# Two decoder layers on one core: small attention matmuls regrouped by the part of the array that they use

## The chip, the cores and the metric

The kernel runs on one core of one Trainium2 chip. The metric is device time in microseconds (us) from the launch to the end of the program; lower is better. Times come from several runs of the same kernel on the chip, and one further execution was recorded by the hardware profiler; the rows below are of that one. The core has a matrix engine (TensorE, PE in the profile, with its weight loads as PEld), a vector engine (DVE), a scalar engine (ACT), GpSimd (POOL) and a sync engine whose queue issues the DMAs (SP).

## What is computed

Two layers of a decoder on 512 prompt tokens and 8 x 4 sample tokens (544 columns in all, width 1024). Each layer is a half-step SwiGLU, a mixer of local attention and gated linear attention (GLA), cross attention to a memory of 256 rows, and a second half-step SwiGLU. The parts that matter here:

```python
def _swa_core(q, kc, vc, sinks, valid):      # 8 q heads, 2 kv heads, head dim 64, window 128
    s = einsum('bnqhgd,bnkhd->bnhgqk', q, kc) * HEAD_DIM ** -0.5
    s = where(valid, s, -inf)
    m = maximum(max(s, axis=-1), sink)
    e = exp(s - m)
    pr = e / (sum(e, axis=-1) + exp(sink - m))
    return einsum('bnhgqk,bnkhd->bnqhgd', pr, vc)

def step(S, inp):                            # GLA, 4 heads, dk 64, dv 128, chunks of 64 tokens
    ...
    A = where(causal, einsum('bhqd,bhkd->bhqk', q_t, k_t), 0.0)
    o = einsum('bhqd,bhdv->bhqv', q_t, S) + einsum('bhqk,bhkv->bhqv', A, vc)
    S_new = exp(b_last)[..., 0, :, None] * S + einsum('bhkd,bhkv->bhdv', k_dec, vc)
    return S_new, o

def cross_attn(h, mk, mv, p):                # 4 heads, head dim 128, 256 memory rows
    q = rms_norm((h @ p['xa_wq']).reshape(B, T, 4, 128), p['xa_q_norm'])
    a = softmax(einsum('bqhd,bkhd->bhqk', q, mk) * 128 ** -0.5)
    return einsum('bhqk,bkhd->bqhd', a, mv).reshape(B, T, 512) @ p['xa_wo']
```

The prompt attends to its own keys; each of the 8 samples has its own key cache, its own GLA state and its own memory keys and values.

## The kernel before

Activations lie transposed, features on the 128 partitions and the 544 tokens along the free axis. The large projections (`product`, line 222, and the feed-forward's `part`, line 447) split every operand in two fp32r halves and run as 128x128 by 272-column matmuls; ACT makes the high half of each weight tile (line 205 or 210) and DVE the low half (206, 211). The attention products are plain fp32; each such `pe.matmul` appears in the trace as two MATMUL records (transposes and fp32r matmuls as one).

The order of the steps in an attention phase is written out by hand in the lists `MIX` (mixer) and `CROSS`; `run` walks through them, and each `yield` in a step gives the next step its turn. The build then places the instructions on the engines by its own estimate of when operands and buffers are ready, so that a step's matmuls can be parted by others in the program that runs. PSUM tiles come from two pools: `psm()` gives a [128, 2, 512] tile of two banks (2 of them), `psa()` a [128, 512] tile of one bank (4 of them). SBUF tiles `big()` hold 4 x 544 columns (9 of them).

The steps that the change touches, all of them small products that use a part of the array's rows (contraction over 64 partitions) or of its columns (an output of 32 or 64 partitions):

- `swa_scores(l, n, kv, ...)`, called by `score n kv` for four windows n and two kv groups. Group kv lies on partitions 64*kv to 64*kv+63 of `qt` and `kt`; the four head blocks j of a group are four matmuls on the same 64 rows (line 536 for n = 0 with 128 columns, 542 else with 256). ACT copies one half of the result (537, 543), DVE masks in the other (538, 544), and then come the softmax, four transposes (565) and one or two masked copies `pt` (569).
- `swa_values`, called by `vals n`: per kv group, and per key block i, one matmul of 512 columns into partitions 64*kv to 64*kv+63 (580).
- `gla_prompt(n)`, called three times by `gla n`: masked products for heads on row half e (797), state updates for token half c (808; DVE adds them up in 815 and 818), and after a yield the outputs: per row half e and pair member i a full matmul with the masked product (834; for n = 0 two half-width ones, 837) and one per token half c with the state (842).
- `sample_scores` (`sscores` in `CROSS`): for each sample b four heads h, accumulated into the 32 columns of b (1237). The memory keys come by DMA, two samples in a `big()` tile (`streamed`, line 1200).
- `sample_values(g)` (`svals g`): for four samples e, two memory halves c, 512 columns each (1255); the values come by `streamed` too, two samples in a tile.

Of the kernel before, what the change touches and what calls it, by code (L numbers as in the profile page):

```python
# [84 lines left out]
def decoder_kernel(  # L85
# [436 lines left out]
        for _ in down(*prev, nxt):  # L522
            pass

    def swa_scores(l, n, kv, qt, kt, fq):


        sink, ns = col[:, l, C_SK + 4 * kv:C_SK + 4 * kv + 4], nsink[:, l, 4 * kv:4 * kv + 4]
        q0 = n * 128
        rows = slice(64 * kv, 64 * kv + 64)  # L530
        s = tmp("s")[:, :512].rearrange("p (j k) -> p j k", j=4)
        prev = km[:, M_PRV:M_PRV + 128].unsqueeze(1).to_broadcast([128, 4, 128])
        if n == 0:
            ps = psm()[:, 0].rearrange("p (j k) -> p j k", j=4)
            for j in range(4):
                pe.matmul(ps[:, j, :], qt[rows, j, 0:128], kt[rows, 0:128], start=True, stop=True)
            act.copy(out=s, in_=ps)
            dve.copy_predicated(out=s, mask=prev, data=neg.unsqueeze(1).to_broadcast([128, 4, 128]))
# [6 lines left out]
        yield 1  # L545
        sm = smp.tile([128, 4, 4], F32, tag="sm", name="sm")
        nm, es, su = sm[:, 0, :], sm[:, 1, :], sm[:, 2, :]
        dve.tensor_reduce(out=es, in_=s, axis=AX.X, op=ALU.max)
        f = fq[:, n, :].rearrange("p (j e) -> p j e", e=2)[:, :, kv]
        dve.scalar_tensor_tensor(out=nm, in0=es, scalar=-1.0, in1=f, op0=ALU.mult, op1=ALU.mult)  # L550
        dve.tensor_tensor(out=nm, in0=nm, in1=ns, op=ALU.min)
# [5 lines left out]
        dve.tensor_tensor(out=es, in0=nm, in1=sink, op=ALU.add)  # L557
# [15 lines left out]
        return out  # L573

    def swa_values(n, pts, vtok, ah, al):
        o = psa()
        for kv in range(2):
            rows = slice(64 * kv, 64 * kv + 64)
# [73 lines left out]
    def mixer(l, nx, nxt):  # L652
# [136 lines left out]
        def gla_prompt(n):  # L789
            st = held["st"]  # L790
            c0 = n * 128
            a = am[n % 2]
            for e in range(2):
                rows = slice(64 * e, 64 * e + 64)
                ps = psa()[:, 0:256].rearrange("p (i t) -> p i t", i=2)
                for i in range(2):
                    pe.matmul(ps[:, i, :], k_t[i][rows, c0:c0 + 128], q_t[i][rows, c0:c0 + 128], start=True, stop=True)
                dve.copy_predicated(
                    out=a[:, 2 * e:2 * e + 2, :],
                    mask=km[:, M_GLA:M_GLA + 128].unsqueeze(1).to_broadcast([128, 2, 128]), data=ps,  # L800
                )
            states = []
            for c in range(2):
                tok = slice(64 * c, 64 * c + 64)
                up = psa()[:, 0:256].rearrange("p (i v) -> p i v", i=2)
                for h in range(4):
                    rows = slice(64 * (h % 2), 64 * (h % 2) + 64)
                    pe.matmul(
                        up[rows, h // 2, :], ktok[tok, n, 64 * h:64 * h + 64], vgt[tok, n, h, :],
                        start=True, stop=True,  # L810
                    )
# [12 lines left out]
            if n == 3:  # L824
                nc.sync.dma_start(out=o_sp[l].rearrange("(i h) d v -> (h d) i v", i=2), in_=st)
            yield 1
            os = []
            for e in range(2):
                rows = slice(64 * e, 64 * e + 64)
                o = psa()[:, 0:256].rearrange("p (i v) -> p i v", i=2)  # L830
                os.append(o)
                for i in range(2):
                    if n > 0:
                        pe.matmul(o[:, i, :], a[:, 2 * e + i, :], vgt[:, n, 2 * i + e, :], start=True, stop=False)  # L834
                    for c in range(2):
                        if n == 0:
                            pe.matmul(
                                o[64 * c:64 * c + 64, i, :], a[:, 2 * e + i, 64 * c:64 * c + 64],
                                vgt[:, n, 2 * i + e, :], start=True, stop=c == 0, tile_position=(0, 64 * c),
                            )  # L840
# [164 lines left out]

        probs = {}

        def scores(n, kv):
            probs[n, kv] = yield from swa_scores(l, n, kv, qt, kt, held["fq"])

        def values(n):
            swa_values(n, [probs[n, 0], probs[n, 1]], vtok, ah, al)
# [145 lines left out]
    def cross(l, nx, nxt):  # L1158
# [70 lines left out]

        def sample_scores():  # L1230
            ps = psa().rearrange("p (g s) -> p g s", g=2)
            for b in range(NB):
                if b % 2 == 0:
                    kt = streamed(cmk_t[l, b // 2], u=4)
                r = slice(32 * (b % 4), 32 * (b % 4) + 32)
                for h in range(4):
                    pe.matmul(  # L1237
                        ps[r, b // 4, :], held["xbd"][:, h, b, :], kt[:, b % 2, h, :], start=h == 0, stop=h == 3,
                        tile_position=(0, 32 * (b % 4)),
                    )  # L1240
# [5 lines left out]
        def sample_values(g):  # L1246
            pts, (oh, ol) = held["sturn"], outs()
            o = psa()
            for e in range(4):
                b = 4 * g + e  # L1250
                if b % 2 == 0:
                    vt = streamed(cmv[l, b:b + 2].rearrange("b (c s) w -> s b c w", c=2), u=2)
                r = slice(32 * e, 32 * e + 32)
                for c in range(2):
                    pe.matmul(  # L1255
                        o[r, :], pts[:, (2 * g + c) * 128 + 32 * e:(2 * g + c) * 128 + 32 * e + 32],
                        vt[:, b % 2, c, :], start=c == 0, stop=c == 1, tile_position=(0, 32 * e),
                    )
            yield 1
            ob = tmp("z")[:, 0:512]  # L1260
# [224 lines left out]
```

## Time and profile before

| | us |
|---|---|
| median of 3 runs | 2222.85 (2221.82 to 2223.49) |
| profiled execution, its own time | 2225.04 |
| span of the profiled execution, first to last instruction | 2223.2 |
| PE busy | 2199.3 (99%) |
| DVE busy | 1567.8 (71%) |
| ACT busy | 1050.1 (47%) |
| mean granted TensorE clock | 0.994 |

The profile's page gives the busy time of each engine, a chain of work followed back from the last instruction, and groups of instructions by line. The chain can be asked for any stretch; its pieces then follow each other without overlap, so a piece's length is the time for which these instructions held up the rest. A busy time of PE also counts the tail of a matmul that overlaps the next one, and is somewhat larger. The two layers show the same picture: mixer and cross attention run from about 400 to 724 us and from about 1500 to 1825 us.

### The profile page before, as it was taken

The page shows a single profiled execution, that of the slowest core. Times are in us where ns is not written, and L with a number is a line of the kernel's source. Part 1 is how long each engine was busy: PE and PEld are TensorE (multiplying, and loading weights), DVE is VectorE, ACT ScalarE, POOL GpSimd, SP SyncE. Part 2 cuts the span into 40 slices and gives each one's busy share as a digit, 9 for nine tenths or more (in the row PEclk, how much of TensorE's full clock was granted, in tenths as well). Part 3 has the DMA queues.
Part 4 walks back from the last instruction along what each step waited for, and adds up shares of the span by engine and source line. Part 5 has one row for each costly group of instructions (what it writes and reads, how often), then busy time and mean ns, then how long its engine had stood idle before and what let it go on. Part 6 is the DMA issues. An engine that isn't in the chain of part 4 may idle for free.

```text
span 2223.2 us, 40766 instructions
## 1 busy us (share of the span) xinstructions
PE 2199.3 (99%) x17250; PEld 2113.1 (95%) x17250; DVE 1567.8 (71%) x2467; ACT 1050.1 (47%) x1721; POOL 7.0 (0%) x17
## 2 busy tenths in 40 slices
PE   8999999999999999999999999999999999999999
PEld 8999999988897999999999999999878979999999
DVE  7987786537654797877679787764476457977874
ACT  6544443535455644444455444435455555444441
POOL 0000000000000000000000000000000000000000
PEclk8999999999999999999999999999999999999999
DMA  4333323322244233233223332333222532333232
GB/s 184 116 94 96 105 86 111 95 75 85 81 149 174 77 105 105 86 105 96 77 85 97 109 91 95 105 100 102 62 87 86 198 116 87 104 97 104 86 101 73
DMA packets 74999, 227.07 MB, mean 102 GB/s; under 512 B 7713, under 2 KB 19745, under 8 KB 73505
## 3 DMA queue, kind: packets, MB, share of 16 engines
q1 hardware_dynamic: 74816, 224.47, 31.6%
q8 instruction: 135, 2.21, 0.4%
q14 instruction: 48, 0.39, 0.1%
HBM read 214.64 MB, written 9.04 MB: 101 GB/s over the span
## 4 chain that ended last, share of the span: by engine, by line
PE 96%; ACT 2%; DVE 1%; DMA 0%; issue 0%; SPq 0%; DVEq 0%; ACTq 0%
PE pm L222 48%; PE pa L447 36%; PE pm L1121 1%; PE pm L1083 1%; PE pm L542 1%; PE pa L580 1%; PE pa L1237 1%; PE pa L1255 1%; PE pa L842 1%; PE pa L1223 1%; PE pa L917 0%; PE pa L834 0%; ACT s L1135 0%; PE pa L565 0%; PE pa L264 0%
## 5 line engine op out<-in xcount | busy, mean ns | idle before, releaser
L222 PE MATMUL pm<-big,hi 128*128 128x272 f32 x5760 | 803.4, 292 | 14.5 <-DVE z L376 10.4
L222 PEld LDWEIGHTS pm<-big,hi 128*128 128x128 f32 x5760 | 757.5, 191 | 21.0 <-issue 13.3
L222 PE MATMUL pm<-big,lo 128*128 128x272 f32 x2880 | 420.5, 289 | 0.0
L222 PEld LDWEIGHTS pm<-big,lo 128*128 128x128 f32 x2880 | 383.0, 188 | 2.1 <-issue 1.2
L205 ACT CAST hi<-raw 128x1024 fp32r<-128x1024 f32 x196 | 205.4, 1049 | 248.6 <-PE pm L222 136.7
L206 DVE TENSOR_TENSOR lo<-raw,hi 128x1024 fp32r<-128x1024 f32 x196 | 238.7, 1218 | 51.9 <-PE pm L222 29.6
L210 ACT CAST hs<-sum 128x1024 fp32r<-128x1024 f32 x152 | 159.9, 1052 | 173.2 <-PE pa L447 143.8
L447 PE MATMUL pa<-t,hs 128*128 128x272 f32 x1368 | 238.7, 289 | 0.0
L447 PE MATMUL pa<-big,hs 128*128 128x272 f32 x1064 | 211.1, 288 | 0.0
L447 PEld LDWEIGHTS pa<-t,hs 128*128 128x128 f32 x1368 | 201.0, 188 | 0.0
L211 DVE TENSOR_TENSOR ls<-sum,hs 128x1024 fp32r<-128x1024 f32 x152 | 185.3, 1219 | 1.8 <-ACT hs L210 0.5
L447 PE MATMUL pa<-big,hi 128*128 128x272 f32 x1216 | 178.7, 289 | 0.0
L387 DVE SCALAR_TENSOR_TENSOR x<-pm,x 128x544 f32<-128x544 f32 x192 | 138.3, 720 | 45.6 <-PE pm L222 45.4
L447 PEld LDWEIGHTS pa<-big,hs 128*128 128x128 f32 x1064 | 166.6, 189 | 0.0
L447 PEld LDWEIGHTS pa<-big,hi 128*128 128x128 f32 x1216 | 163.0, 188 | 0.0
L447 PE MATMUL pa<-t,ls 128*128 128x272 f32 x912 | 153.0, 290 | 0.0
L447 PEld LDWEIGHTS pa<-t,ls 128*128 128x128 f32 x912 | 129.7, 189 | 0.0
L210 ACT CAST hi<-raw 128x1024 fp32r<-128x1024 f32 x76 | 80.1, 1054 | 96.5 <-PE pm L222 84.7
L210 ACT CAST hd<-raw 128x512 fp32r<-128x512 f32 x76 | 47.2, 621 | 138.0 <-PE pa L447 131.5
L447 PE MATMUL pa<-big,lo 128*128 128x272 f32 x608 | 109.5, 288 | 0.0
L433 DVE TENSOR_TENSOR sum<-raw 128x512 f32<-128x512 f32 x152 | 98.2, 686 | 12.7 <-DMA raw<-in_wts_dram 12.7
L433 DVE TENSOR_TENSOR sum<-sum,raw 128x512 f32<-128x512 f32 x152 | 104.2, 686 | 0.0
(303 smaller groups left out, 2609.3 us busy)
## 6 DMA issues: line engine op xcount, KB each, us to landing
raw<-in_wts_dram SPq DMA_DIRECT2D x348, 512.0 KB
big<-in_cmk_t_dram SPq DMA_DIRECT2D x8, 1024.0 KB
big<-in_cmv_dram SPq DMA_DIRECT2D x8, 1024.0 KB
kc<-in_consts_dram SPq DMA_DIRECT2D x2, 1546.0 KB
x<-in_x_dram SPq DMA_DIRECT2D x8, 272.0 KB
z<-big SPq DMA_DIRECT2D x32, 68.0 KB
out_dram<-x SPq DMA_DIRECT2D x8, 272.0 KB
cache<-in_s_dram SPq DMA_DIRECT2D x8, 256.0 KB
```

The lines of the kernel that those rows point to most:

```text
L205: act.copy(out=hi, in_=raw)
L206: dve.tensor_tensor(out=lo, in0=raw, in1=hi.bitcast(F32), op=ALU.subtract)
L210: act.copy(out=hi, in_=src)
L211: dve.tensor_tensor(out=lo, in0=src, in1=hi.bitcast(F32), op=ALU.subtract)
L222: pe.matmul(ps[:, h, :s.stop - s.start], w, x[:, s], start=i == 0, stop=i == len(steps) - 1)
L387: dve.scalar_tensor_tensor(out=x, in0=p, scalar=scale, in1=x, op0=ALU.mult, op1=ALU.add)
L433: dve.tensor_tensor(out=t[:, e], in0=t[:, 0] if x is None else x, in1=y, op=ALU.add)
L447: pe.matmul(ps, u, v, start=first and i == 0, stop=i == len(steps) - 1, skip_group_check=not first)
L542: pe.matmul(ps[:, j, :], qt[rows, j, q0:q0 + 128], kt[rows, q0 - 128:q0 + 128], start=True, stop=True)
L580: pe.matmul(o[rows, :], vtok[:, n - i, rows], p, start=i == 0, stop=i == len(pts[kv]) - 1)
L842: pe.matmul(o[64 * c:64 * c + 64, i, :], q_t[i][rows, c0 + 64 * c:c0 + 64 * c + 64], states[c][rows, i, :], start=False, stop=True, tile_p ...
L1083: pe.matmul(pk[:, h, :], w[:, o:o + 128], x[:, k, :], start=st and h % 2 == 0, stop=sp and h % 2 == 1)
```

## The change

Five places, with the same operands and results:

- `swa_scores` takes a pair of head blocks w in place of a kv group: blocks 2w and 2w+1, each for both kv groups e. Its four matmuls alternate between row halves 0 to 63 and 64 to 127, and e picks the PSUM bank. The factors, sinks and the copies after it are addressed accordingly; for n = 0 the tile takes both banks.
- `swa_values` makes twice as many matmuls of 256 columns, alternating between the column halves.
- `gla_prompt` issues the masked products alternating between row halves; the state updates alternate between token halves and column halves; in the outputs both row halves' tiles `os` are taken first, and for each i the full matmuls of both e come first, then the four with the states.
- `sample_scores` takes the key tiles of four samples first, then goes over heads h with the four samples inside, each on its own 32 columns.
- `sample_values` takes both value tiles first, then goes over c with the four samples inside.

```diff
-    def swa_scores(l, n, kv, qt, kt, fq):
+    def swa_scores(l, n, w, qt, kt, fq):
...
+        ps = psm().rearrange("p e (j k) -> p j e k", j=2)
+        for j in range(2):
+            for e in range(2):
+                rows = slice(64 * e, 64 * e + 64)
+                pe.matmul(
+                    ps[:, j, e, 0:q0 + 128 - k0], qt[rows, 2 * w + j, q0:q0 + 128], kt[rows, k0:q0 + 128],
+                    start=True, stop=True,
+                )
         if n == 0:
-            ps = psm()[:, 0].rearrange("p (j k) -> p j k", j=4)
-            for j in range(4):
-                pe.matmul(ps[:, j, :], qt[rows, j, 0:128], kt[rows, 0:128], start=True, stop=True)
-            act.copy(out=s, in_=ps)
+            act.copy(out=s, in_=ps[:, :, :, 0:128])
...
         else:
-            ps = psm().rearrange("p a (j k) -> p (a j) k", j=2)
-            for j in range(4):
-                pe.matmul(ps[:, j, :], qt[rows, j, q0:q0 + 128], kt[rows, q0 - 128:q0 + 128], start=True, stop=True)
-            act.copy(out=s, in_=ps[:, :, 128:256])
-            dve.copy_predicated(out=s, mask=prev, data=ps[:, :, 0:128])
+            act.copy(out=s, in_=ps[:, :, :, 128:256])
+            dve.copy_predicated(out=s, mask=prev, data=ps[:, :, :, 0:128])
...
     def swa_values(n, pts, vtok, ah, al):
         o = psa()
-        for kv in range(2):
-            rows = slice(64 * kv, 64 * kv + 64)
-            for i, p in enumerate(pts[kv]):
-                pe.matmul(o[rows, :], vtok[:, n - i, rows], p, start=i == 0, stop=i == len(pts[kv]) - 1)
+        for w in range(2):
+            for i, p in enumerate(pts[w]):
+                for kv in range(2):
+                    rows = slice(64 * kv, 64 * kv + 64)
+                    pe.matmul(
+                        o[rows, 256 * w:256 * w + 256], vtok[:, n - i, rows],
+                        p.rearrange("p (j e q) -> p e j q", j=2, e=2)[:, kv], start=i == 0, stop=i == len(pts[w]) - 1,
+                    )
...
-            for e in range(2):
-                rows = slice(64 * e, 64 * e + 64)
-                ps = psa()[:, 0:256].rearrange("p (i t) -> p i t", i=2)
-                for i in range(2):
+            halves2 = [slice(0, 64), slice(64, 128)]
+            pss = [psa()[:, 0:256].rearrange("p (i t) -> p i t", i=2) for _ in range(2)]
+            for i in range(2):
+                for ps, rows in zip(pss, halves2):
                     pe.matmul(ps[:, i, :], k_t[i][rows, c0:c0 + 128], q_t[i][rows, c0:c0 + 128], start=True, stop=True)
...
-            os = []
-            for e in range(2):
-                rows = slice(64 * e, 64 * e + 64)
-                o = psa()[:, 0:256].rearrange("p (i v) -> p i v", i=2)
-                os.append(o)
-                for i in range(2):
+            os = [psa()[:, 0:256].rearrange("p (i v) -> p i v", i=2) for _ in range(2)]
+            for i in range(2):
+                for e, o in enumerate(os):
                     if n > 0:
                         pe.matmul(o[:, i, :], a[:, 2 * e + i, :], vgt[:, n, 2 * i + e, :], start=True, stop=False)
...
+                for c, tok in enumerate(halves2):
+                    for e, o in enumerate(os):
                         if states[c] is not None:
                             pe.matmul(
-                                o[64 * c:64 * c + 64, i, :], q_t[i][rows, c0 + 64 * c:c0 + 64 * c + 64],
-                                states[c][rows, i, :], start=False, stop=True, tile_position=(64 * e, 64 * c),
+                                o[tok, i, :], q_t[i][halves2[e], c0 + 64 * c:c0 + 64 * c + 64],
+                                states[c][halves2[e], i, :], start=False, stop=True, tile_position=(64 * e, 64 * c),
                             )
...
-            for b in range(NB):
-                if b % 2 == 0:
-                    kt = streamed(cmk_t[l, b // 2], u=4)
-                r = slice(32 * (b % 4), 32 * (b % 4) + 32)
+            for g in range(2):
+                kt = [streamed(cmk_t[l, 2 * g + i], u=4) for i in range(2)]
                 for h in range(4):
-                    pe.matmul(
-                        ps[r, b // 4, :], held["xbd"][:, h, b, :], kt[:, b % 2, h, :], start=h == 0, stop=h == 3,
-                        tile_position=(0, 32 * (b % 4)),
-                    )
+                    for e in range(4):
+                        pe.matmul(
+                            ps[32 * e:32 * e + 32, g, :], held["xbd"][:, h, 4 * g + e, :], kt[e // 2][:, e % 2, h, :],
+                            start=h == 0, stop=h == 3, tile_position=(0, 32 * e),
+                        )
...
-            for e in range(4):
-                b = 4 * g + e
-                if b % 2 == 0:
-                    vt = streamed(cmv[l, b:b + 2].rearrange("b (c s) w -> s b c w", c=2), u=2)
-                r = slice(32 * e, 32 * e + 32)
-                for c in range(2):
+            vt = [
+                streamed(cmv[l, 4 * g + i:4 * g + i + 2].rearrange("b (c s) w -> s b c w", c=2), u=2) for i in (0, 2)
+            ]
+            for c in range(2):
+                for e in range(4):
                     pe.matmul(
...
```

## Rows read from the trace of the kernel before

**Rows 1.** The page: busy time by engine; the chain that ended last, by engine.
```profile
PE 2199.3 (99%) x17250; PEld 2113.1 (95%) x17250; DVE 1567.8 (71%) x2467; ACT 1050.1 (47%) x1721; POOL 7.0 (0%) x17
...
PE 96%; ACT 2%; DVE 1%; DMA 0%; issue 0%; SPq 0%; DVEq 0%; ACTq 0%
```

**Rows 2.** PE groups by line: shapes, count, busy us, mean ns, idle before.
```profile
L542 PE MATMUL pm<-kt,big 64*128 64x256 f32 x96 | 24.2, 389 | 0.0
L580 PE MATMUL pa<-pt,vtok 128*64 128x512 f32 x56 | 20.2, 611 | 0.0
...
L1237 PE MATMUL pa<-big,cache 128*32 128x256 f32 x128 | 16.3, 382 | 0.0
...
L1255 PE MATMUL pa<-big,pt 128*32 128x512 f32 x64 | 15.3, 599 | 0.8 <-ACT pt L1152 0.8
```

**Rows 3.** Chain in order of time (start us, us, what), 410 to 505.
```profile
413.20 1.97 PE pa L693 x32
...
465.81 0.65 PE pa L797 x8
...
468.80 0.61 PE pa L808 x16
...
498.80 0.64 PE pa L797 x4
```

**Rows 4.** Chain, 517 to 541: the local scores of layer 0.
```profile
517.43 1.49 PE pm L542 x6
...
523.22 0.86 PE pm L536 x6
...
525.95 0.63 PE pm L542 x2
...
527.74 1.16 PE pm L536 x8
528.90 1.73 PE pm L542 x8
...
538.41 1.92 PE pm L542 x8
```

**Rows 5.** Chain, 562 to 589: local values.
```profile
562.16 1.87 PE pa L580 x8
...
585.44 1.00 PE pa L580 x2
...
587.03 1.87 PE pa L580 x6
```

**Rows 6.** Chain, 475 to 482: GLA outputs, n = 0 and then n = 1.
```profile
475.21 0.37 PE pa L837 x4
475.58 0.36 PE pa L842 x2
...
478.13 0.42 PE pa L834 x2
478.55 0.36 PE pa L842 x4
...
481.90 0.22 PE pa L834 x2
```

**Rows 7.** Chain, 679 to 707: cross attention of the samples.
```profile
679.75 8.10 PE pa L1237 x64
...
700.62 1.92 PE pa L1255 x8
...
704.46 1.85 PE pa L1255 x8
```

**Rows 8.** Stretches: busy us by engine, granted clock, DMA share, GB/s.
```profile
515.00:580.00 65.00, 64.26 (x463) 52.60 (x462) 48.65 (x128) 40.26 (x119) 0.00 (x0) 1.00 0.24 70
690.00:708.00 18.00, 17.35 (x108) 12.70 (x106) 11.08 (x22) 14.74 (x41) 0.00 (x0) 1.00 0.80 291
```

**Rows 9.** SP's queue, 660 to 700: issue of the samples' memory values.
```profile
692.60 3.31 SPq L1200 DMA_DIRECT2D big<-in_cmv_dram  x4
```

More of the change, by code (lines that the diff above doesn't have):

```diff
@@ L523, in ffn @@
             pass
[L525 to L544 removed]
+    def swa_scores(l, n, w, qt, kt, fq):
+        sink, ns = (
+            c.rearrange("p (e j) -> p j e", e=2)[:, 2 * w:2 * w + 2]
+            for c in (col[:, l, C_SK:C_SK + 8], nsink[:, l, 0:8])
+        )
+        q0 = n * 128
+        k0 = max(q0 - 128, 0)
+        s = tmp("s")[:, :512].rearrange("p (j e k) -> p j e k", j=2, e=2)
+        prev = km[:, M_PRV:M_PRV + 128].unsqueeze(1).unsqueeze(1).to_broadcast([128, 2, 2, 128])
+        ps = psm().rearrange("p e (j k) -> p j e k", j=2)
[6 more added lines that the diff above has]
+                )
+        if n == 0:
+            act.copy(out=s, in_=ps[:, :, :, 0:128])
+            dve.copy_predicated(
+                out=s, mask=prev, data=neg.unsqueeze(1).unsqueeze(1).to_broadcast([128, 2, 2, 128])
+            )
+        else:
+            act.copy(out=s, in_=ps[:, :, :, 128:256])
+            dve.copy_predicated(out=s, mask=prev, data=ps[:, :, :, 0:128])
         yield 1
+        s = s.rearrange("p j e k -> p (j e) k")
         sm = smp.tile([128, 4, 4], F32, tag="sm", name="sm")
@@ L548, in swa_scores @@
         dve.tensor_reduce(out=es, in_=s, axis=AX.X, op=ALU.max)
-        f = fq[:, n, :].rearrange("p (j e) -> p j e", e=2)[:, :, kv]
+        f = fq[:, n, 4 * w:4 * w + 4]
         dve.scalar_tensor_tensor(out=nm, in0=es, scalar=-1.0, in1=f, op0=ALU.mult, op1=ALU.mult)
-        dve.tensor_tensor(out=nm, in0=nm, in1=ns, op=ALU.min)
+        nm3, es3 = (t.rearrange("p (j e) -> p j e", e=2) for t in (nm, es))
+        dve.tensor_tensor(out=nm3, in0=nm3, in1=ns, op=ALU.min)
         for j in range(4):
@@ L556, in swa_scores @@
             )
-        dve.tensor_tensor(out=es, in0=nm, in1=sink, op=ALU.add)
+        dve.tensor_tensor(out=es3, in0=nm3, in1=sink, op=ALU.add)
         act.activation(out=es, in_=es, func=AF.Exp)
@@ L576, in swa_values @@
         o = psa()
-        for kv in range(2):
-            rows = slice(64 * kv, 64 * kv + 64)
-            for i, p in enumerate(pts[kv]):
-                pe.matmul(o[rows, :], vtok[:, n - i, rows], p, start=i == 0, stop=i == len(pts[kv]) - 1)
+        for w in range(2):
[5 more added lines that the diff above has]
+                        p.rearrange("p (j e q) -> p e j q", j=2, e=2)[:, kv], start=i == 0, stop=i == len(pts[w]) - 1,
+                    )
         q = slice(n * 128, n * 128 + 128)
@@ L792, in gla_prompt @@
             a = am[n % 2]
[L793 to L796 removed]
+            halves2 = [slice(0, 64), slice(64, 128)]
+            pss = [psa()[:, 0:256].rearrange("p (i t) -> p i t", i=2) for _ in range(2)]
+            for i in range(2):
+                for ps, rows in zip(pss, halves2):
                     pe.matmul(ps[:, i, :], k_t[i][rows, c0:c0 + 128], q_t[i][rows, c0:c0 + 128], start=True, stop=True)
+            for e, ps in enumerate(pss):
                 dve.copy_predicated(
@@ L802, in gla_prompt @@
             states = []
-            for c in range(2):
[L804 to L807, printed above, removed]
-                    pe.matmul(
-                        up[rows, h // 2, :], ktok[tok, n, 64 * h:64 * h + 64], vgt[tok, n, h, :],
-                        start=True, stop=True,
-                    )
+            ups = [psa()[:, 0:256].rearrange("p (i v) -> p i v", i=2) for _ in range(2)]
+            for i in range(2):
+                for up, tok in zip(ups, halves2):
+                    for e, rows in enumerate(halves2):
+                        h = 2 * i + e
+                        pe.matmul(
+                            up[rows, i, :], ktok[tok, n, 64 * h:64 * h + 64], vgt[tok, n, h, :],
+                            start=True, stop=True,
+                        )
+            for c, up in enumerate(ups):
                 states.append(st)
@@ L826, in gla_prompt @@
             yield 1
-            os = []
-            for e in range(2):
-                rows = slice(64 * e, 64 * e + 64)
-                o = psa()[:, 0:256].rearrange("p (i v) -> p i v", i=2)
-                os.append(o)
-                for i in range(2):
+            os = [psa()[:, 0:256].rearrange("p (i v) -> p i v", i=2) for _ in range(2)]
+            for i in range(2):
+                for e, o in enumerate(os):
                     if n > 0:
                         pe.matmul(o[:, i, :], a[:, 2 * e + i, :], vgt[:, n, 2 * i + e, :], start=True, stop=False)
-                    for c in range(2):
-                        if n == 0:
+                    else:
+                        for c, tok in enumerate(halves2):
                             pe.matmul(
-                                o[64 * c:64 * c + 64, i, :], a[:, 2 * e + i, 64 * c:64 * c + 64],
-                                vgt[:, n, 2 * i + e, :], start=True, stop=c == 0, tile_position=(0, 64 * c),
-                            )
+                                o[tok, i, :], a[:, 2 * e + i, tok], vgt[:, n, 2 * i + e, :],
+                                start=True, stop=c == 0, tile_position=(0, 64 * c),
+                            )
+                for c, tok in enumerate(halves2):
+                    for e, o in enumerate(os):
                         if states[c] is not None:
                             pe.matmul(
-                                o[64 * c:64 * c + 64, i, :], q_t[i][rows, c0 + 64 * c:c0 + 64 * c + 64],
-                                states[c][rows, i, :], start=False, stop=True, tile_position=(64 * e, 64 * c),
+                                o[tok, i, :], q_t[i][halves2[e], c0 + 64 * c:c0 + 64 * c + 64],
+                                states[c][halves2[e], i, :], start=False, stop=True, tile_position=(64 * e, 64 * c),
                             )
@@ L1006, in mixer, with scores @@
         probs = {}
-        def scores(n, kv):
-            probs[n, kv] = yield from swa_scores(l, n, kv, qt, kt, held["fq"])
+        def scores(n, w):
+            probs[n, w] = yield from swa_scores(l, n, w, qt, kt, held["fq"])
         def values(n):
@@ L1248, in sample_values @@
             o = psa()
-            for e in range(4):
-                b = 4 * g + e
-                if b % 2 == 0:
-                    vt = streamed(cmv[l, b:b + 2].rearrange("b (c s) w -> s b c w", c=2), u=2)
-                r = slice(32 * e, 32 * e + 32)
-                for c in range(2):
+            vt = [
[3 more added lines that the diff above has]
+                for e in range(4):
                     pe.matmul(
-                        o[r, :], pts[:, (2 * g + c) * 128 + 32 * e:(2 * g + c) * 128 + 32 * e + 32],
-                        vt[:, b % 2, c, :], start=c == 0, stop=c == 1, tile_position=(0, 32 * e),
+                        o[32 * e:32 * e + 32, :], pts[:, (2 * g + c) * 128 + 32 * e:(2 * g + c) * 128 + 32 * e + 32],
+                        vt[e // 2][:, e % 2, c, :], start=c == 0, stop=c == 1, tile_position=(0, 32 * e),
                     )
```

4 lines of the change are left out of this document (2 added, 2 removed).

## The prediction, made before the change was run

> **What bounds the kernel now.** I read the page first: PE is busy for 99% of the span, and the chain that ended last consists of PE for 96% [rows 1]. So a microsecond of PE saved is a microsecond of the end, as long as the neighbours keep up. Next the PE groups by line, to size what is touched: 542, 580, 1237 and 1255 are 76 us of busy PE in both layers [rows 2]; with the smaller lines of the same steps it comes, by the parts below, to some 56 us per layer, 5% of the span in all. More than that can't be had, and a part must stay.
>
> Last the chain in order of time, where lengths don't overlap. The reader is to see two things in it. First, matmuls on different parts of the array already run beside each other. Eight records of line 797, four on each row half, take 0.65 us, and four on one half, where the build had parted them, 0.64 us [rows 3]: the second half costs nothing. Sixteen of line 808, on four quarters, take 0.61 us. Line 693, whose loop already has the new form (the column quarter changes with every matmul, each with a stream of its own), runs 32 records of 272 columns in 1.97 us, that is 0.06 us each, while a score record of 256 columns on a single row half takes 0.215 us ((1.92 - 1.49) / 2) [rows 3, 4]. Second, this overlap reaches only a little ahead: line 1237, with eight records on one quarter before the next, takes 8.10 / 64 = 0.127 us a record, about two at a time and not four; the scores, eight on one half, take 1.92 us, none beside another [rows 4, 7]. What is to be had is thus the difference between what already overlaps and what could.
>
> **A step's price.** Call a step the time that one record of a part needs: 0.215 us for 256 columns; for 512 columns four steps take 1.87 us and two take 1.00, so 0.435 a step; for 128 columns 0.11 (the 0.22 of two records in line) [rows 4 to 6]. A group adds about 0.2 us once for its start and its end (1.92 - 8 x 0.215) [rows 4].
>
> **Part by part, per layer.**
>
> Scores. Six calls with n > 0: four of 1.92, one of 1.73 right behind its neighbour, one in pieces of 1.49 and 0.63 because its fourth head block was not yet there; 11.5 us. Two with n = 0: 1.16, and 0.86 for six of eight records; 2.2 us [rows 4]. After: four steps in pairs, 4 x 0.215 + 0.2 = 1.06 us, and 0.65 for n = 0, the very shape of line 797 [rows 3]. 6 x 1.06 + 2 x 0.65 = 7.7 us, so 6.1 are saved. The two heads go to different PSUM banks, as line 797's do. ACT's and DVE's work after it is the same in count and size. The first call no longer needs the fourth block.
>
> Values. Before, one whole call of 1.87 (pairs already), two in pieces of 1.00 and 1.87, because the later probabilities come late, and n = 0 in two pieces of 1.00: 9.6 us [rows 5]. After, halves of 256 columns always in pairs: a whole call is 8 steps, 8 x 0.215 + 0.2 = 1.92, no gain; in pieces it is 0.63 for two steps and 1.49 for six, the rows of that length [rows 4], 2.12; n = 0 is 2 x 0.63. 1.26 + 1.92 + 2 x 2.12 = 7.4: 2.2 saved; 0.8 if every probability block makes a piece of its own, 2.8 if none does. I take 2.2, as the same blocks come late as before.
> The Trainium skill speaks against this edit: "TensorEngine Tiling (Array Packing)", Performance Considerations, Instruction Overhead, gives each matmul some 60 cycles and warns against splitting an already small side. At 2.4 GHz that would be 25 ns for each of the 56 added records, an estimate of 1.4 us in both layers, and the saving here would fall from 4.4 to 3.0. The trace has 8 x 0.215 against 4 x 0.435 and shows no such price.
>
> GLA outputs. For n = 0 four rounds of 0.37 + 0.36, 2.9 us; for n = 1 to 3 four of 0.42 + 0.36, 3.1 us each [rows 6]. Most of a round is the price of changing the form: two 128-column records take 0.22 in line with others of their form and 0.42 between different ones. After, there are two rounds. n > 0: four full records, 0.42 + 2 x 0.11 = 0.64, and eight on four quarters, two steps, 0.61 - 2 x 0.11 = 0.39 [rows 3, 6]; 2 x 1.03 = 2.06. n = 0: 0.37 + 0.22 and then two row halves, 0.37: 2 x 0.96 = 1.9. Saved 1.0 + 3 x 1.05 = 4.2; if the wait for the second state parts two of the rounds, 3.4.
>
> GLA products and updates. Both overlap where they stand together [rows 3], so the new order gives nothing; the one parted product can save 0.6, but both PSUM tiles are now wanted at once: 0 to 0.6, I take 0.3.
>
> Sample scores. 64 records in 16 steps of four: 16 x 0.215 + 0.2 = 3.6 us in place of 8.10 [rows 7]; by line 693's pace, 2 x 1.97 = 3.9. Saved 4.2 to 4.5, I take 4.4. A group now waits for two key tiles; all four were used in one unbroken run, so they were there, and SP issues the same transfers in the same order.
>
> Sample values. Two calls, each in two groups of eight that already run in pairs, 1.92 + 1.85 [rows 7]. All sixteen as four steps of four would take 1.87: 3.7 saved for both. But the groups stand 3.8 us apart, since the second tile comes later: the four transfers are issued from 692.6 to 695.9 and move at some 300 GB/s, 3.5 us for each MB [rows 8, 9]. The build will probably place two samples, let others pass and then do the other twelve records: 1.00 + 1.87 for 3.77 [rows 5]. So 1.7 saved, between 0 (same two groups as now) and 3.7. If PE does wait there for the second tile, the turns and values of the prompt's heads (1150, 1223) are queued behind it, and ACT's copies of the turns wait for those.
>
> Sum 6.1 + 2.2 + 4.2 + 0.3 + 4.4 + 1.7 = 18.9 per layer.
>
> **What is late next.** From 515 to 580, where the scores lie, DVE is busy for 48.65 of 65 us and ACT for 40.26 [rows 8]. With about 8 us less PE, DVE stands at 85%; it still has slack, but single waits of the softmax appear: I take off 0.75. From 690 to 708 ACT has 14.74 of 18 us, and the exponentials, not PE, lead the chain there; of the sample values' saving I take off 1.0. The sample scores lie ahead of it and shift it as a whole. Leaves 17.1 per layer, 34 for two. Against the profiled execution's own 2225.04 us that is 2191; it ran 2.2 us over the median, so the median comes to 2222.85 - 34 = 2188.5, rounded 2188.
>
> **Rivals.**
> Much of the saved PE time is waited away: the probabilities, ACT in the cross attention and the second tile decide instead. Then scores keep 4 of 6, sample values none, the rest two thirds: 4 + 7.4 = 11.4 per layer, 2200; with 2 us of idle PE more in each, 2204. For it: ACT's share from 690 on. Against it: nearly no idle PE from 515 to 580 (0.74 us), and products of line 222 as filler.
> More than forecast: values whole, the sixteen records together, nothing lost; 21.9 per layer, 2179.
> The change doesn't do what it says: the build parts the new groups again by its own estimates, so that partners don't meet. Only the sample scores and outputs gain, 5 to 7 per layer, 2209 to 2213. For it: it parted scores, values and products in the trace. Against: their partners now become ready together.
> Slower: changing the part drains the array, as changing the form does. Then each of some 230 alternations (64 matmuls in the scores, 56 in the values, 64 in the samples' scores, some 50 elsewhere) costs the 0.2 us of a group's start and end, 46 us, and with no overlap gained it comes to some 2270. With the overlap it decides from 34 / 230 = 0.15 us a change on, where it eats the saving. Line 693 changes the quarter at each matmul and has 0.06 us a record in all [rows 3], so this would need the row halves to act otherwise than the quarters; line 797 speaks against that too.
>
> **How the numbers follow.** Chances: forecast with its bounds (2180 to 2197) 0.66; waited away 0.17; more than forecast 0.07; parted again 0.06; slower 0.04. The range leaves out the slow case, the parted one and the ends: 2178 to 2204. A difference of under 0.2% (4.4 us) can't be told from none here. Faster takes everything but the slow case and a little of the two weak ones: 0.93; same 0.03; slower 0.04.
>
> **What would show it.** In the chain: score groups of eight at about 1.06 us and 0.65; sample scores 64 records in about 3.6; a GLA output round at 1.03; values never over 2.2 a call. Idle PE from 515 to 580 and from 690 to 708 should grow by some 1 to 2 us per layer. The forecast is wrong if the groups keep their lengths (alternating doesn't pair), if they shrink but the ends of the phases don't move (waits on ACT or DVE), or if the granted clock, 1.00 in these stretches [rows 8], falls.

## The result, and the profile after

The changed kernel takes 2198.43 us (median; 2196.03 to 2201.33), the kernel before, run beside it, 2222.89 (2221.82 to 2223.49). The ratio is 0.9892, with a 95% interval of 0.9879 to 0.9904: 24.5 us less, 1.1%. Forecast were 34 less, 2188, with a range of 2178 to 2204. Direction and range held; ten microseconds of the forecast did not come.

The profiled executions are 2225.04 us before and 2198.65 after (span 2196.6). First the page of after, the lines that answer [rows 1]: busy time by engine, and the chain that ended last by engine.

```profile
PE 2167.0 (99%) x17306; PEld 2097.3 (95%) x17306; DVE 1567.6 (71%) x2467; ACT 1049.6 (48%) x1721; POOL 7.0 (0%) x17
...
PE 95%; DVE 2%; ACT 2%; DMA 1%; issue 1%; SPq 0%; DVEq 0%; ACTq 0%
```

PE's busy time fell by 32 us, DVE's and ACT's not at all: the work between the matmuls is the same. PE is still the bound, but DVE and DMA have a larger share of the chain (DVE 1% to 2%, DMA 0% to 1%). The groups by line that answer [rows 2] (lines 541, 591, 1251 and 1268 are the former 542, 580, 1237 and 1255; 541 also holds the former 536, another form):

```profile
L591 PE MATMUL pa<-pt,vtok 128*64 128x256 f32 x112 | 15.2, 392 | 0.0
L541 PE MATMUL pm<-kt,big 64*128 64x256 f32 x96 | 14.8, 400 | 0.0
L1268 PE MATMUL pa<-big,pt 128*32 128x512 f32 x64 | 10.8, 601 | 0.7 <-ACT pt L1167 0.7
...
L1251 PE MATMUL pa<-big,cache 128*32 128x256 f32 x128 | 7.3, 380 | 0.0
```

One record takes as long as before (400 ns for a score, 389 before), and yet the group is 14.8 us in place of 24.2: more of them run beside each other. The chain of after (start us, us, what) shows the single calls. Scores and values, layer 0:

```profile
535.84 1.06 PE pm L541 x6
...
537.48 0.62 PE pm L541 x2
...
546.38 0.58 PE pa L591 x4
...
547.50 1.06 PE pm L541 x8
...
581.01 0.58 PE pa L591 x4
...
582.18 1.45 PE pa L591 x12
```

A whole score call is 1.06 us, 1.92 before [rows 4]; six records alone still take 1.06. A values call in pieces is 0.58 + 1.45, before 1.00 + 1.87 [rows 5]. The samples in the cross attention:

```profile
673.60 3.59 PE pa L1251 x64
...
694.93 1.85 PE pa L1268 x16
...
700.30 1.84 PE pa L1268 x12
```

64 score records in 3.59 us where there were 8.10 [rows 7].

All parts of the change, each line's matmuls added up from the start of one to the start of the next in the trace, in us per layer (the mean of the two):

| | before | after | saved | forecast |
|---|---|---|---|---|
| local scores | 13.7 | 8.4 | 5.3 | 6.1 |
| local values | 9.6 | 7.1 | 2.5 | 2.2 |
| GLA outputs | 12.5 | 9.8 | 2.7 | 4.2 |
| GLA products and updates | 5.7 | 5.6 | under 0.1 | 0.3 |
| sample scores | 8.1 | 3.6 | 4.5 | 4.4 |
| sample values | 7.4 | 5.2 | 2.2 | 1.7 |
| sum | 57.0 | 39.7 | 17.3 | 18.9 |

So 34.6 us went from the parts in both layers, and yet the layers became only 14.7 and 13.2 us shorter (from the first matmul of the gate, line 707, to that of the second feed-forward; 28.0 together; the start-up was 1.4 longer in this execution, so that the span is 26.6 shorter). What was lost, was lost in the mixers: up to the first matmul of the cross attention they are 7.5 and 5.8 us shorter where their lines give 10.7 and 10.4. It lies at one place, ahead of the local scores. PE at 520 us, with its idle time before the instruction in brackets:

```profile
520.26 0.45 PE L798 MATMUL pa<-ident,z 128*128 128x128 f32 x1 [2.30 <-DVE z L793]
```

The transposes of the last GLA normalisation wait for DVE, 2.3 us here and 3.7 in layer 1; before, the same stretch has one wait, on another step:

```profile
PE pa L264 <- ACT u L398: 0.7, 1, 0.7
```

Why DVE is late is seen in its own order, first after, then before (971 to 973 and 956 to 958 are the last rotation, 790 and 793, or 776 and 779, the normalisation):

```profile
517.87 0.18 DVE L790 RECIPROCAL sm<-sm 128x4 f32<-128x4 f32 x1 [2.77 <-ACT sm L789]
518.42 0.72 DVE L972 TENSOR_TENSOR z<-z,kc 128x544 f32<-128x544 f32 x1 [0.37 <-DMA z<-big]
519.06 0.72 DVE L973 TENSOR_TENSOR big<-big,kc 128x544 f32<-128x544 f32 x1
519.70 0.75 DVE L793 TENSOR_TENSOR z<-pa,sm 128x256 f32<-128x256 f32 x2
```

```profile
518.46 0.18 DVE L776 RECIPROCAL sm<-sm 128x4 f32<-128x4 f32 x1 [3.35 <-ACT sm L775]
518.75 0.76 DVE L779 TENSOR_TENSOR z<-pa,sm 128x256 f32<-128x256 f32 x2
519.42 0.72 DVE L957 TENSOR_TENSOR z<-z,kc 128x544 f32<-128x544 f32 x1
```

The build has put the rotation, which first waits for a DMA, ahead of the normalisation, whose factors were ready (518.05, the end of line 790) before that DMA landed. In layer 1 the rotation waits 1.83 us for its DMA in that place, and the normalisation behind it is so much later. And there is a second loss behind the wait. Stretches of after: busy us of PE, PEld, DVE, ACT and POOL, then the granted clock:

```profile
520.00:525.00 5.00, 4.68 (x27) 1.96 (x28) 4.29 (x11) 1.97 (x5) 0.00 (x0) 0.66 0.01 3
1605.00:1610.00 5.00, 1.93 (x10) 0.87 (x10) 3.77 (x10) 0.00 (x0) 0.00 (x0) 0.56 0.42 121
1610.00:1615.00 5.00, 5.00 (x36) 2.63 (x35) 3.61 (x7) 3.69 (x8) 0.00 (x0) 0.76 0.00 0
```

From 520 to 525 PE is busy and gets 0.66 of its clock: for part of the stretch it was granted the half level, 1.2 GHz. That is 0.34 x 5 = 1.7 us of lost work. In the kernel before these stretches had 1.00.

### The profile page after: what moved, and what is told of

The parts are those of the page before. It is cut to its first block, busy times and chain, and to the rows that moved or that the text cites. A ratio compares the mean times of both kernels' runs of the same rounds, so it can differ in the third digit from the quotient of the medians.

```text
span 2196.6 us, 40872 instructions
## 1 busy us (share of the span) xinstructions
PE 2167.0 (99%) x17306; PEld 2097.3 (95%) x17306; DVE 1567.6 (71%) x2467; ACT 1049.6 (48%) x1721; POOL 7.0 (0%) x17
## 4 chain that ended last, share of the span: by engine, by line
PE 95%; DVE 2%; ACT 2%; DMA 1%; issue 1%; SPq 0%; DVEq 0%; ACTq 0%
PE pm L222 48%; PE pa L447 36%; PE pm L1136 1%; PE pm L1098 1%; PE pa L1238 1%; PE pa L264 0%; PE pa L591 0%; PE pm L541 0%; PE pa L1268 0%; PE pm L1221 0%; PE pa L575 0%; PE pa L857 0%; PE pa L1251 0%; DMA out_dram<-state 0%; DVE lo L206 0%
## 5 line engine op out<-in xcount | busy, mean ns | idle before, releaser
L222 PE MATMUL pm<-big,hi 128*128 128x272 f32 x5760 | 804.9, 292 | 15.1 <-DVE z L376 10.4
```

The lines of the kernel that those rows point to most:

```text
L222: pe.matmul(ps[:, h, :s.stop - s.start], w, x[:, s], start=i == 0, stop=i == len(steps) - 1)
```

## The experiments

Four kernels split the change by its parts; two set the order on DVE by hand; one tests the pairing, one the parted outputs. Each stands against the kernel before run on the same chip.

**e1_cross**: before, with the two parts of the cross attention only.

```diff
 # sample_scores, sample_values as changed; swa_scores, swa_values, gla_prompt as before
+            for g in range(2):
+                kt = [streamed(cmk_t[l, 2 * g + i], u=4) for i in range(2)]
...
+            for c in range(2):
+                for e in range(4):
```

> Only the two sample steps of the cross attention in the new order. Theory S (the parts add up, each worth what its groups shrink by): the 64 sample-score records take 3.6 us in place of 8.1 and the sample values lose some 2.2 us of PE per layer, nothing is given back, so 13 to 14 us less than before. Rival W (ACT's exponentials after 690 us decide): only the sample scores count, 9 us less.

2213.41 us, ratio 0.9952 (0.9936 to 0.9969), 10 less. The 64 sample scores are one piece of 3.59 us. The mixers are as before to 0.01 us, so the cross attention gives 5 us per layer, between the two expectations and nearer to the lower: not all that the groups shrink by is kept. In layer 0 their lines give 6.3 us (8.1 to 3.6, and 7.4 to 5.65), and from the first matmul of the cross attention to that of the second feed-forward the layer is 5.2 shorter (154.4 for 159.6). The values come in pieces of 4 and 12 records, as they were forecast.

**e2_local**: before, with scores and values of the local attention only.

```diff
 # swa_scores, swa_values as changed; the rest as before
-    def swa_scores(l, n, kv, qt, kt, fq):
+    def swa_scores(l, n, w, qt, kt, fq):
```

> Only the local scores and values in the new order. In this build DVE still does the last GLA normalisation ahead of the last rotation, as before. Theory O (the wait of 2.3 and 3.8 us before the last normalisation's transposes in the changed kernel comes from the rotation being placed ahead of the normalisation on DVE): no such wait here, and the whole 5.3 + 2.5 us per layer are kept, 15 to 16 us less. Rival F (PE merely has less work left to fill the time until the last rotation's DMA lands): the wait comes here too, 1 to 2 us per layer, and 11 to 13 us less.

2209.74 us, ratio 0.993 (0.9912 to 0.9948), 13.7 less. From the gate to the cross attention's first matmul each layer is 7.8 us shorter (205.66 for 213.41), of 8.7 that the two lines give in this kernel (scores 13.7 to 7.55, values 9.6 to 7.1). There is no wait of over 0.7 us from 480 to 600: these parts don't cause the new one. That is theory O's picture, though its 15 to 16 us were not reached.

**e3_gla**: before, with the change of `gla_prompt` only.

```diff
 # gla_prompt as changed; the rest as before
+            for i in range(2):
+                for e, o in enumerate(os):
```

> Only the GLA steps in the new order. In this build DVE does the last rotation ahead of the last normalisation, as in the changed kernel. Theory O: PE's groups save 2.6 us per layer, but PE waits some 2 us per layer before the normalisation's transposes, so 0 to 3 us less in all. Rival F: the old, longer scores still fill the time, no wait, 5 us less.

2238.61 us, ratio 1.0063 (1.0041 to 1.0085): 15 us slower than before. Neither expectation had that. PE's waits from 505 to 560 (who, for whom, us in total, times, longest), and the two stretches of low clock:

```profile
PE pm L222 <- ACT s L537: 2.5, 1, 2.5
PE pa L784 <- DVE z L779: 1.9, 1, 1.9
```

```profile
520.00:525.00 5.00, 5.00 (x20) 1.73 (x15) 2.63 (x7) 2.43 (x6) 0.00 (x0) 0.50 0.00 0
535.00:540.00 5.00, 4.99 (x27) 4.96 (x27) 5.00 (x17) 1.01 (x4) 0.00 (x0) 0.66 0.03 8
```

The rotation stands ahead of the normalisation here too, PE waits, and the clock falls with each wait, to half for a full stretch of 5 us at the first. This profiled execution is 9 us longer than that of before (span 2232.4 against 2223.2), 8.0 of them in layer 0's mixer; two of the runs took some 2242 us.

**e8_no_gla**: the changed kernel with `gla_prompt` as before.

```diff
 # swa_scores, swa_values, sample_scores, sample_values as changed
-            os = [psa()[:, 0:256].rearrange("p (i v) -> p i v", i=2) for _ in range(2)]
+            os = []
```

> The changed kernel with the GLA steps in the old order; DVE keeps the normalisation ahead of the rotation. Theory O and S: 13.5 + 15.5 = 29 us less than before, so some 3 us faster than the whole change although a part of it is missing. Rival F: the wait stays, and the missing 2.6 us per layer make it slower than the whole change, 20 us less than before.

2197.18 us, ratio 0.9878 (0.9863 to 0.9893), 26.3 less: as fast as the whole change. The GLA part thus gave nothing in sum, and the other four give their own sum, 10 + 13.7 = 23.8, and a little more. Theory O's picture holds; its 29 us were not reached, and rival F's 20 are not met either. The wait on line 793 is 0.2 us.

**after_again**: the changed kernel once more, beside the next ones.

> The changed kernel once more, beside the next ones on the same chip: 2196 to 2201 us, a wait of PE before the last normalisation's transposes in both mixers, and a granted clock under 1.00 in the stretch behind it.

2196.98 us, ratio 0.9888 (0.9872 to 0.9905). The wait is there again, 2.3 and 3.0 us, with one difference: in layer 0 the clock stayed at 1.00 from 520 to 525, and this layer's mixer was 1.4 us shorter than in the first execution (204.5 against 205.9 us from the gate to the cross attention's first matmul). The wait comes with the program; the fall of the clock behind it doesn't follow each time.

**e4_norm_first**: the changed kernel with one order set by hand: the last rotation's two DVE products are issued behind the last normalisation.

```diff
-    "glas, states, rot 3, gla 3, rot 4, gla 3, qf, qf, score 1 0, ..."
+    "glas, states, rot 3, gla 3, gla 3, rot 4, qf, qf, score 1 0, ..."
...
-                dve.tensor_tensor(
+                held["normed"] = dve.tensor_tensor(
...
-            dve.tensor_tensor(out=t, in0=t, in1=sin, op=ALU.mult)
-            dve.tensor_tensor(out=dst, in0=dst, in1=cos, op=ALU.mult)
+            with tc.issue_after(held["normed"].ins) if i == 4 else nullcontext():
+                dve.tensor_tensor(out=t, in0=t, in1=sin, op=ALU.mult)
+                dve.tensor_tensor(out=dst, in0=dst, in1=cos, op=ALU.mult)
```

> The changed kernel with one edge of order on DVE: the last rotation's two products behind the last GLA normalisation. Theory O (the wait comes from DVE's order, and the lower clock from the wait): the wait falls from 2.3 and 3.8 us to under 1 us, the granted clock stays at 1.00 in both mixers, and with the 10.2 us of half clock there worth 5 us the time falls by some 9 us to 2189. Rival F (the last rotation's DMA and what hangs on it set the time): the wait only moves behind the scores of the last head block, 2195 to 2199.

2193.31 us, ratio 0.9869 (0.9854 to 0.9883): the lowest median of these kernels, 28.9 less than before and 3.7 less than after_again beside it. That is less than half of the 9 us that theory O expected, and the interval overlaps that of e8_no_gla. The wait, alike in both layers, and a stretch of each:

```profile
PE pa L798 <- DVE z L793: 0.8, 1, 0.8
```

```profile
520.00:525.00 5.00, 4.97 (x43) 2.88 (x39) 4.95 (x12) 3.37 (x9) 0.00 (x0) 1.00 0.00 0
1605.00:1610.00 5.00, 4.97 (x42) 2.54 (x38) 4.36 (x11) 2.56 (x5) 0.00 (x0) 1.00 0.04 8
```

The wait is 0.8 us and the clock stays full. From the gate to the cross attention's first matmul both layers take 202.95 us, 10.5 less than before (213.41), of 11.1 that the mixer's lines give in this kernel (5.9 + 2.5 + 2.7). After had 205.9 and 207.7 there, and after_again, with the wait of 2.3 us and the full clock, 204.5 in layer 0: 1.5 us more than here, which is the difference of the two waits. Two of the 7.7 us won against after are given back behind it, in the cross attention of layer 0. The chain of e4_norm_first there:

```profile
690.82 1.84 PE pa L1269 x12
692.66 3.04 PE pm L222 x24
695.70 0.98 PE pa L1269 x4
```

The build lets 24 records of line 222 pass between the two calls of sample values; the four records then stand alone (0.98 us), and the waits listed from 685 to 712 have 0.5 us for weight halves of line 222 that after has not. In after the four followed at once, sixteen records in 1.85 us. e1_cross has the same order here as e4_norm_first (1.84, 3.04, 0.98).

**e9_gla_norm_first**: e3_gla with the same order set by hand.

> Only the GLA steps in the new order, with the same edge of order on DVE. Theory O: the loss of 15 us that the GLA steps alone showed comes from the order of DVE and ACT behind them and the lower clock; with the edge the 2.6 us of PE per layer remain, 4 to 6 us less than before. Rival G (the new GLA order is slower in itself, by the two PSUM tiles that it holds): 8 to 15 us more than before, as without the edge.

2219.58 us, ratio 0.9986 (0.9976 to 0.9995), 2.6 less than before, where e3_gla was 15 more. Rival G is out; theory O's 4 to 6 were not reached, though each mixer is 2.1 us shorter than before (211.30 for 213.41) in the traces. The wait on the normalisation is 0.3 us, and the stretches from 515 to 530 have a clock of 1.00. One order on DVE makes some 18 us between two kernels with the same matmuls, each taken against its own runs of before.

**e5_not_alternating**: the changed kernel, but in a score call both blocks of row half 0 come first, then both of half 1.

```diff
-        for j in range(2):
-            for e in range(2):
+        for e in range(2):
+            for j in range(2):
```

> The changed kernel with the score loops exchanged: both blocks of row half 0, then both of row half 1, two banks as before. Theory Q (the engine reaches some records ahead, as in line 797 of the kernel before, and pairs what lies four records apart): a score call still takes 1.06 us and 0.65 for n = 0. Rival N (only neighbouring matmuls pair): 1.5 us or more, two of the four steps being alone.

One execution, 2196.49 us. A whole score call in its chain:

```profile
545.15 1.07 PE pm L541 x8
```

1.07 us against 1.06. It isn't the alternation of neighbours that pairs the halves: with four records (two matmuls) on one half before four on the other they still overlap in full. In the kernel before, all eight records of a call lay on one half, and in its chain no call of the other half stands next to one; a call took 1.92. That the heads of both groups stand in one call is what counts here.

**e10_outputs_pm**: e4_norm_first, with the two results of the GLA outputs in the two banks of one `psm` tile. **e4_again** ran beside it.

```diff
-            os = [psa()[:, 0:256].rearrange("p (i v) -> p i v", i=2) for _ in range(2)]
+            op = psm()
+            os = [op[:, e, 0:256].rearrange("p (i v) -> p i v", i=2) for e in range(2)]
```

> This is the kernel e4_norm_first with one more edit: the GLA outputs' two results lie in the two banks of one psm tile in place of two psa tiles. T, the rounds of n = 1 and 2 are parted by row half because the second psa tile isn't free when the first is: with one psm tile for both, a round of n = 1 to 3 shows whole in the chain, four records of line 848 in about 0.64 and eight of line 858 in about 0.38 us. n = 1 then loses 1.1 us and n = 2 about 0.5, 1.6 per layer, 3 in all against e4_norm_first: about 2190. D, the tile is gained at the cost of line 222, which also writes psm tiles and fills the gaps of this stretch: the rounds are whole but PE waits for masked products, states or normalisations where line 222 stood; 2196 to 2203.

> The kernel of e4_norm_first once more, beside e10_outputs_pm on the same chip: 2193 within 2 us, score calls of 1.06 us, and one wait of 0.8 us on the last normalisation in each layer.

e4_again: 2191.83 us, ratio 0.986 (0.9845 to 0.9875). e10_outputs_pm: 2202.97, ratio 0.991 (0.9893 to 0.9926), 11 us slower than it. The chain of e10_outputs_pm at n = 2, and PE's waits from 455 to 600:

```profile
481.50 0.45 PE pm L848 x4
481.95 0.38 PE pm L858 x8
482.33 0.64 PE pm L848 x4
482.97 0.38 PE pm L858 x8
```

```profile
PE pm L222 <- ACT s L546: 3.8, 1, 3.8
PE pa L798 <- DVE z L793: 2.1, 1, 2.1
```

The rounds for n = 1 to 3 are whole, as both expectations have it (the outputs take 8.5 us per layer where after needs 9.8), and the time is D's, at its upper end, not T's 2190. Line 222 fills this stretch otherwise and needs the same `psm` tiles; now it waits 3.8 us for ACT to copy a score result (546), and PE waits 2.1 us for the normalisation again, with a clock of 0.67 from 520 to 525. Here the order on DVE is not the reason: the normalisation stands ahead of the rotation (517.89 and 519.59). A gain of 1.3 us per layer on the outputs brought a loss; 9.6 us of it lie in layer 0's mixer (212.55 for 202.97 in e4_again).

Both heads' scores in one PSUM bank were not tried.

## Why the prediction was right, and where it was not

**Scores: right, once nothing disturbs them.** Forecast 7.7 us per layer, 8.4 in after, 7.8 in e4_norm_first. The length of a call held to 0.01 (1.06). One reading behind it was no proof: that the scores of before run one by one doesn't show how far the overlap reaches, as no call of the other half stood next to theirs. Of the two examples given only line 1237 shows it. The rest in after is scores that ran at the half clock (a call of 1.10 in layer 1) and a call parted into 1.06 + 0.62 in both layers.

**Values: right, a little better.** Pieces of 0.58 and 1.45 where the prediction had 0.63 and 1.49; the parting is the one that it assumed. The price that the Trainium skill's "TensorEngine Tiling (Array Packing)", Performance Considerations, Instruction Overhead, gives each added matmul doesn't show: four steps of 256 columns take 0.87 us (1.45 - 0.58), as two of 512 did (1.87 - 1.00), and 2.5 us were saved per layer against 2.2 without it.

**GLA outputs: the mis-sized term, 2.7 of 4.2.** The prediction priced a round at 1.03 and had whole rounds for n = 1 to 3. n = 0 came as forecast (1.9), and n = 3 has whole rounds, of 0.64 + 0.38. For n = 1 the chain of after reads as that of before [rows 6]; the first two lines here are n = 0:

```profile
476.55 0.59 PE pa L850 x8
477.13 0.36 PE pa L857 x4
...
478.45 0.42 PE pa L847 x2
478.87 0.37 PE pa L857 x4
...
480.02 2.21 PE pm L222 x16
482.23 0.22 PE pa L847 x2
482.45 0.37 PE pa L857 x4
```

First row half 0, then 2.2 us of line 222, then half 1: the build parted the pair, and n = 1 cost 1.0 us more than forecast. n = 2 cost 0.8 more; it is parted, as before the change, between the two states of its first result. e10_outputs_pm points to the tiles: with both results in one tile the rounds of n = 1 and 2 come whole. For what the second tile waited in after, no run shows. The prediction let only a late second state part a round (3.4 as its low end). That both PSUM tiles are wanted at once it wrote of the products, and took no loss for the outputs, which have the same need.

**GLA products: right that little was to be had.** The parted one is still parted, 0.64 and 0.64, and nothing was won.

**Sample scores: right**, 3.59 us against 3.6. **Sample values: right in its likely case.** 1.00 + 1.87 per call were forecast, 0.98 + 1.84 stand in e4_norm_first (5.65 per layer, 1.75 saved). After has 5.65 in layer 1 and 4.7 in layer 0, where the second call's first four ran behind the first call's twelve. The reason given, a late second tile, is only partly right, for the transfers come earlier than in [rows 9]. SP issues the values' tiles in after at

```profile
682.14 3.29 SPq L1215 DMA_DIRECT2D big<-in_cmv_dram  x4
```

4.9 us after the last sample score as before (4.8), but 10.5 us earlier in time, while the first group of eight or more starts only 5.7 us earlier. By the records of the transfers' ends in the trace of after, the four tiles of layer 0 are in at 689.5, 692.0, 694.6 and 697.1; the first call's four records start at 690.0 and its twelve at 694.9, so the second tile was missing at the four, as the prediction had it. In e4_norm_first the second call is parted as well, four at 695.6 and twelve at 698.5, though its tiles were in at 690.7 and 693.3: there the order that the build chose parts the call, not the transfer.

Of the 1.0 us per layer taken off for ACT, nothing shows in layer 0 of after: from the cross attention's first matmul to the feed-forward it is 7.2 us shorter, as much as its two lines give. In layer 1 it is 7.5 shorter where the lines give 6.3, but up to 1.7 of that is the clock at the start of the second feed-forward (before 0.86, 0.50 and 0.96 in the stretches from 1855 to 1870, after 0.92 and 0.73 from 1830 to 1840). Where the order of the samples' values is the other one, about a microsecond does go: layer 0 keeps 5.2 of 6.3 us in e1_cross and 5.4 of 6.3 in e4_norm_first, with the same loss by the clock in each. So the size was right there; how much of it is ACT's, no run here shows.

**What is late next: the wrong place and too little.** The prediction took off 0.75 us per layer for softmax waits between 515 and 580. What came late was the step just ahead of the first score, the last normalisation. Its waits, 2.3 and 3.7 us, were not among the rivals. Here the last rotation and the normalisation are ready on DVE close to each other (518.4 and 518.05 in layer 0 of after, 1606.2 and 1604.4 in layer 1), the build puts one ahead by its own estimate, and no line of the change touches either. e3_gla and e9_gla_norm_first, which differ by the order set by hand alone, show that it makes or removes the loss; why the build's estimate flipped, no run shows. It is not the only way to a late normalisation: e10_outputs_pm has the right order and waits 2.1 us. e2_local and e8_no_gla, where `gla_prompt` is the old one, have the old order.

**The clock: the prediction had it as a way to be wrong, without a price.** It is 1.7 us in layer 0 and (0.44 + 0.24) x 5 = 3.4 in layer 1 by the stretches shown, a part of which lies within the wait itself. In layer 0, wait (2.3 - 0.8) and clock (1.7) make 3.2 us; the mixer is 2.95 longer than in e4_norm_first. In layer 1 the wait (3.7 - 0.8) and at most 3.4 make up to 6.3, and it is 4.7 longer.

**The sum.** Forecast 37.8 from the parts, less 3.5 for waits: 34. By the profiled executions 34.6 from the parts, less 6.6 that the two layers did not keep, less 1.4 at the start, which also varies between executions of one kernel: 26.6 of span, or 26.4 by the executions' own times. The 6.6 are 7.8 lost in the mixers, less 1.2 that the cross attention is ahead of its lines, by the clock in layer 1. The medians have 24.5, as the execution profiled before was 2.2 over its median and the one after 0.2. So two thirds of the gap to the forecast lie in the parts and the waits, some 3.2 us each, and the rest is start-up and the spread of single executions. The prediction also has a slip of a third of a microsecond: 2222.85 - 34 is 2188.85, not 2188.5. That the range held is in part luck, for the loss that filled it was not the one that had been priced. The rival "waited away" (2200) had about the right amount and the wrong reason: it let ACT, the probabilities and the second tile decide, and what decided in after was DVE's order and the clock.

## What to carry to other kernels

Matmuls on different parts of the array overlapped here when a partner stood within four records, and the step price read from one line predicts another to some per cent; so put partners into one group, and see that all the PSUM tiles that the group needs at once are really free. When PE work is taken from a stretch, look at the last step that PE needs ahead of it on DVE and at what else becomes ready there in the same microsecond: an order that was right by chance can flip and cost more than the edit gives, and an order set by hand can bring it back. Try each part of a change alone: here the GLA part was worth nothing, or a loss, until that order was set, and some 2.6 us in the whole with it.

## What was not expected of the hardware

- A wait of PE of about 2 to 3 us can cost nearly as much again: the granted clock was at the half level for part of the microseconds around its end and behind it (0.66 over 5 us at 2.3 us in after, 0.50 at 1.9 us in e3_gla), yet stayed at 1.00 behind the same 2.3 us in after_again, and behind 0.8 us in e4_norm_first. The kernel before shows it too at the start of the second feed-forward, 0.71 from 760 to 765 behind a wait of 2.8 us.
- The overlap reaches over four records on one half of the array (e5_not_alternating, 1.07 us). Over eight records on one quarter it is only partial: 64 sample-score records took 8.10 us before, and 3.59 when every matmul changes the quarter. For eight records on a row half no run here has the test.
